# The last layer norm of a transformer block: the end of the feed-forward product in two fresh PSUM banks of 256 columns, and one of its four column blocks normalised by TensorE and ScalarE

## Chip, cores and metric

The kernel runs on one core of a Trainium2 chip. The metric is the device time of one execution in microseconds (us), median over the runs; lower is better. The engines are TensorE (PE in the profile; PEld is its weight load), VectorE (DVE), ScalarE (ACT), GpSimd (POOL) and SyncE (SP). SP, ACT and POOL also issue transfers (DMAs) from their queues.

## What is computed

One block of a hybrid network on 256 tokens of width 2048: a gated delta rule and a sparse attention, merged, then a layer norm, a gated feed-forward part of width 5632 and a second layer norm. Only the end is touched:

```python
x = layer_norm(DEEPNORM_ALPHA * x + merged @ w_out[l], ln1_g[l], ln1_b[l])
h_gate, h_up = jnp.split(x @ w_ffn_in[l], 2, axis=-1)
x = layer_norm(DEEPNORM_ALPHA * x + (jax.nn.silu(h_gate) * h_up) @ w_ffn_out[l], ln2_g[l], ln2_b[l])

def layer_norm(x, g, b):
    mu = mean(x); var = mean(square(x - mu))        # over the 2048 columns
    return (x - mu) * rsqrt(var + 1e-5) * g + b
```

Everything is f32. The large products are made of three matmuls in fp32r each: an operand is split into a high part and a rest, and hi*hi, hi*lo and lo*hi are summed.

## The kernel before

The 256 tokens are two blocks `tb` of 128 rows (partitions). The result of the second product (hidden 256 x 5632 times `w_ffn_out` 5632 x 2048) is made in two groups `g` of 1024 columns, each of two halves `n` of 512 columns; a group has four PSUM banks `bank[2 * tb + n]`. `x1[tb]` (128 x 2048, in SBUF) holds the residual and takes the sums; `out_block(tb, g, n)` is its block of 512 columns `2 * g + n`. So each row of the result has four column blocks of 512, numbered `j` from 0 to 3.

The 44 contraction tiles of 128 come as 22 pairs `q`. `chunk` (L79 to L86) loads a piece of weights of 128 x 1024 from SP's queue (L81), ScalarE casts it to `hi` (L83), and VectorE subtracts to get `lo` (L85). `mm3` (L206 to L209) is the three matmuls. Some pairs go through `seven_pair`, which makes seven products where eight would be, from forms that VectorE builds (L240 to L255); their sums are put into `x1` by `seven_chain` (L1003 to L1021) on VectorE, a step at each `tick`. The other pairs go through `plain_pair`. TensorE's and SP's order is the order of the program as written. On the other engines a scheduler sets the order by its own costs, and `tc.high_priority` moves what stands under it ahead.

In the second group the last four pairs (`HELD = 4`) are held: their products for token block 0 run first, those for token block 1 afterwards, half `n = 0` and then half `n = 1`, so that the norm of token block 0 runs on VectorE while TensorE makes block 1. The end reads:

```python
for n in range(2):                                  # L1338
    add_out(0, 1, n, bank[n])
ln2(0)
for n in range(2):
    for q, cks in held:
        for j in range(2):
            plain(bank, cks, hh_, hl_, q, j, n, 1, q == FT // 2 - 1)
    add_out(1, 1, n, bank[2 + n])
ln2(1)                                              # L1346
```

`add_out` (L1023 to L1028) adds a bank to its block of `x1` (L1025) and takes the statistics of that block (L1028, `bn_stats`, six numbers per row and block). `ln` (L1086 to L1108) aggregates them to mean and variance (`mv`, L1099), adds epsilon (`ve`, L1101), lets GpSimd raise that to the power -0.5 (`rs`, in `rsqrt`, L412), and makes for each block j two passes on VectorE: `first` (L1089), (x - mean) * gamma, and `second` (L1094), x * rs + beta. The first pass of block 0 stands ahead of `ve` in VectorE's order. Each finished block is stored at once, 256 KB, from ACT's queue for even j and SP's for odd j (L1335). `ln2_t` are four tiles of 128 x 1024 with gamma (0 and 1) and beta (2 and 3), broadcast to all rows by GpSimd's queue (L1306) during the second group.

Of the kernel before, what the change touches and what calls it, by code (L numbers as in the profile page):

```python
# [8 lines left out]
F32 = mybir.dt.float32  # L9
# [46 lines left out]
def block_kernel(ctx: ExitStack, tc: tile.TileContext, xT, x, cpack, onehot, relb, convw, alog, dtb, gnw,  # L56
# [162 lines left out]
        cs = slice(n * 512, (n + 1) * 512)  # L219
        mm3(bank[2 * tb + n], sh[:, k, ts], sl[:, k, ts], hi[:, cs], lo[:, cs], q == 0 and j == 0, last and j == 1)  # L220

    def plain_pair(bank, src, sh, sl, q, last):
        cks = pair_chunks(src, q)
        for j in range(2):
            for n in range(2):
                for tb in range(NTB):
                    plain(bank, cks, sh, sl, q, j, n, tb, last)
            tick()

    def seven_pair(bank, wbank, src, sh, sl, q, form, home, first, last):  # L230
# [46 lines left out]
    padp = ctx.enter_context(tc.tile_pool(name="padp", bufs=1, side="right"))  # L277
    pad = padp.tile([P, 24], F32, name="pad")
    nc.vector.memset(pad, 0.0)
    pads = sm.tile([P, 16], F32, name="pads")  # L280
    nc.vector.memset(pads, 0.0)
    xs_ = ExitStack()
    xpool = xs_.enter_context(tc.tile_pool(name="xp", bufs=1, side="right"))
# [714 lines left out]
    def out_block(tb, g, n):  # L998
        j = 2 * g + n
        return x1[tb][:, j * 512:(j + 1) * 512]  # L1000
# [22 lines left out]
    def add_out(tb, g, n, ps):  # L1023
        v = out_block(tb, g, n)
        nc.vector.tensor_add(v, v, ps)  # L1025
        if 2 * g + n == 0:
            stats[tb] = sm.tile([P, 4, 6], F32, name="stats", tag="stats", bufs=2)
        nc.vector.bn_stats(stats[tb][:, 2 * g + n, :], v)  # L1028

    def load_x():  # L1030
# [55 lines left out]
    def ln(tb, gt, bt, after, ahead=(0, 0, 0)):  # L1086
        def first(j):
            v = x1[tb][:, j * 512:(j + 1) * 512]
            nc.vector.scalar_tensor_tensor(v, v, mv[:, 0:1], gt[:, j * 512:(j + 1) * 512],  # L1089
                                           op0=OP.subtract, op1=OP.mult)  # L1090

        def second(j):
            v = x1[tb][:, j * 512:(j + 1) * 512]
            nc.vector.scalar_tensor_tensor(v, v, rs, bt[:, j * 512:(j + 1) * 512], op0=OP.mult, op1=OP.add)  # L1094
            after(j, v)

        with tc.high_priority(offset=ahead[0]):
            mv = sm.tile([P, 2], F32, name="mv", tag="mv", bufs=2)
            nc.vector.bn_aggr(mv, stats[tb].rearrange("p a b -> p (a b)"))  # L1099
            ve = sm.tile([P, 1], F32, name="ve", tag="ve", bufs=2)  # L1100
            nc.vector.tensor_scalar(ve, mv[:, 1:2], LN_EPS, None, op0=OP.add)  # L1101
            rs = sm.tile([P, 1], F32, name="rs", tag="rs", bufs=2)
            rsqrt(rs, ve, hv)
            first(0)
        with tc.high_priority(offset=ahead[1]):
            second(0)
        with tc.high_priority(offset=ahead[2]):
            for j in (1, 2, 3):  # L1108
                first(j)
                second(j)  # L1110
# [156 lines left out]
    def group(g, ps_std, ps_w, n):  # L1267
        nonlocal wq, mp_
        bank = [ps_std() for _ in range(4)]
        for q in range(n):  # L1270
            if not g and q == 2:
                finish()
                for i in OUT_AT:
                    h_tile(hp2, i)
                for tb in range(NTB):
                    x1[tb] = rp.tile([P, D], F32, name=f"x1_{tb}", tag=f"x1_{tb}")
                xs_.close()
                mp_ = fh.enter_context(tc.tile_pool(name="mp", bufs=1, side="right", reuse_waits="tile"))
                wq = wqs.enter_context(tc.tile_pool(name="wq", bufs=2, side="left", reuse_waits="tile"))
                for tag in ("tlo", "thi", "wt", "gt", "wraw"):  # L1280
                    wq_tile(tag)
            if q == WQ[g][0]:
                wbank = [ps_w() for _ in range(4)]
            if g and q in LN2_LOAD:
                ln2_load(LN2_LOAD.index(q))
            if not g and q in FETCH:
                fetch(OUT_AT[0] + FETCH.index(q) // 2, FETCH.index(q) % 2)
            if not g and 15 <= q < 19:
                c, tb = divmod(q - 15, 2)
                cs = slice(c * 1024, c * 1024 + 1024)  # L1290
                nc.sync.dma_start(x1[tb][:, cs], d_x1[tb, :, cs])
            if q in WQ[g]:
                seven_pair(bank, wbank, wfo[g], hh_, hl_, q, streamed, wq_tile, q == WQ[g][0], q == WQ[g][-1])
                if q == WQ[g][-1]:
                    start(seven_chain(g, wbank, mp_.tile([P, 512], F32, name="wm", tag="wm")))
            else:
                plain_pair(bank, wfo[g], hh_, hl_, q, q == FT // 2 - 1)
        return bank


# [12 lines left out]
    bank = group(1, ps_acc, ps_aux, FT // 2 - HELD)  # L1313
    wqs.close()
    ex2 = fh.enter_context(tc.tile_pool(name="ex2", bufs=4, side="left", reuse_waits="tile"))
    held = []
    for q in range(FT // 2 - HELD, FT // 2):
        cks = pair_chunks(wfo[1], q, ex2 if q < FT // 2 - HELD // 2 else None)
# [15 lines left out]
    def ln2(tb):  # L1334
        ln(tb, Halves(*ln2_t[:2]), Halves(*ln2_t[2:]), lambda j, v: (nc.sync if j % 2 else nc.scalar).dma_start(  # L1335
            out[tb * P:(tb + 1) * P, j * 512:(j + 1) * 512], v))

    for n in range(2):  # L1338
        add_out(0, 1, n, bank[n])
    ln2(0)  # L1340
    for n in range(2):
        for q, cks in held:
            for j in range(2):
                plain(bank, cks, hh_, hl_, q, j, n, 1, q == FT // 2 - 1)
        add_out(1, 1, n, bank[2 + n])
    ln2(1)  # L1346
    assert not chains
    fh.close()

# [106 lines left out]
```

## Time and profile before

| | before |
|---|---|
| median of 3 runs | 1463.47 us (1463.41 to 1463.56) |
| profiled execution | span 1462.0 us; its whole time is not recorded apart |
| TensorE busy | 1447.7 us, 99% of the span |
| VectorE, ScalarE, GpSimd busy | 1219.6, 797.0, 45.8 us |
| granted TensorE clock, mean | 0.998 |
| last store issued | 1458.74 us from the span's start |

Times in the rows of the profile count from the start of the span, which is the first to the last instruction of one execution; the runs' times also hold what lies around it. A row of the timeline is the start, the duration, the engine, the line of the source, the operation, output <- inputs and the shapes; in brackets stands how long the engine was idle before and what ended that. Rows of groups give the count, the busy time in us and the mean of one in ns. The duration of a matmul includes its way through the array, so one starts before the one ahead of it has ended.

### The profile page before, as it was taken

Reading aid. Unit: us, or ns where it says so; the run is one execution under the profiler, and the core shown is the slowest. Engines: PE = TensorE matmul, PEld = TensorE weight load, DVE = VectorE, ACT = ScalarE, POOL = GpSimd, SP = SyncE. Lnnn points to the kernel's source line nnn. Section 1 sums busy time; section 2 is a strip of 40 time slices with the busy share of each in tenths; the row PEclk is TensorE's granted clock in tenths of the full one; section 3 lists DMA queues with packets and bytes.
Section 4 is the critical chain, followed back from the end, with each engine's and each line's share of the span. In section 5 each row is a group of like instructions: output and inputs, shape, how many; then the busy total and the mean of one; then the engine's idle time right before and its main releaser. Section 6 shows DMA issues by size and latency. Waiting matters only on the chain.

```text
span 1462.0 us, 19399 instructions
## 1 busy us (share of the span) xinstructions
PE 1447.7 (99%) x7146; PEld 1217.9 (83%) x7146; DVE 1219.6 (83%) x1654; ACT 797.0 (55%) x982; POOL 45.8 (3%) x58
## 2 busy tenths in 40 slices
PE   9999999999999999999999999999999999999996
PEld 9888888888888888888888888888888888888885
DVE  6798985468489678879886799989999998989887
ACT  6765443346466445545534565656566565554551
POOL 0002010030000000000000000000000000000000
PEclk9999999999999999999999999999999999999999
DMA  8646675444556565567856767666666667888853
GB/s 295 195 155 194 185 180 169 152 135 147 186 184 217 182 208 193 185 185 245 292 182 207 239 232 245 206 211 204 228 203 211 218 215 248 311 335 267 325 199 115
DMA packets 93407, 310.16 MB, mean 212 GB/s; under 512 B 16688, under 2 KB 17624, under 8 KB 92544
## 3 DMA queue, kind: packets, MB, share of 16 engines
q1 hardware_dynamic: 82176, 290.11, 59.5%
q0 software_dynamic: 4096, 16.45, 3.5%
q10 hardware_dynamic: 7040, 2.36, 0.7%
q8 instruction: 56, 0.92, 0.3%
q14 instruction: 39, 0.32, 0.1%
HBM read 295.05 MB, written 13.83 MB: 211 GB/s over the span
## 4 chain that ended last, share of the span: by engine, by line
PE 95%; DVE 2%; DMA 1%; issue 1%; ACT 1%; SPq 0%; POOLq 0%; DVEq 0%; ACTq 0%
PE acc L145 10%; PE acc L208 10%; PE acc L209 10%; PE acc L207 10%; PE aux L207 9%; PE aux L209 9%; PE aux L208 9%; PE acc L148 5%; PE acc L167 5%; PE acc L166 5%; PE acc L165 5%; PE aux L672 1%; PE aux L165 1%; PE aux L167 1%; PE aux L166 1%
## 5 line engine op out<-in xcount | busy, mean ns | idle before, releaser
L83 ACT CAST hi<-raw 128x1024 fp32r<-128x1024 f32 (+1 forms) x391 | 405.8, 1045 | 392.1 <-PE acc L167 88.2
L85 DVE TENSOR_TENSOR lo<-raw,hi 128x1024 fp32r<-128x1024 f32 (+1 forms) x391 | 473.8, 1220 | 148.0 <-ACT hi L83 145.1
L145 PE MATMUL acc<-X,hi 128*128 128x512 f32 x640 | 203.7, 399 | 0.0
L148 PEld LDWEIGHTS acc<-X,lo 128*128 128x128 f32 x640 | 120.2, 188 | 28.3
L207 PE MATMUL acc<-hi,X 128*128 128x512 f32 x364 | 142.2, 391 | 0.0
L209 PE MATMUL acc<-hi,X 128*128 128x512 f32 x364 | 141.7, 389 | 0.0
L208 PE MATMUL acc<-lo,X 128*128 128x512 f32 x364 | 141.7, 389 | 0.0
L207 PE MATMUL aux<-hi,X 128*128 128x512 f32 x332 | 129.9, 391 | 0.6 <-DVE ol__108 L852 0.6
L209 PE MATMUL aux<-hi,X 128*128 128x512 f32 x332 | 129.3, 389 | 0.0
L208 PE MATMUL aux<-lo,X 128*128 128x512 f32 x332 | 129.2, 389 | 0.0
L148 PE MATMUL acc<-X,lo 128*128 128x256 f32 x640 | 126.0, 278 | 0.0
L145 PEld LDWEIGHTS acc<-X,hi 128*128 128x128 f32 x640 | 97.5, 189 | 2.0 <-ACT hi L83 0.7
L240 ACT CAST f_thi<-f_wt 128x1024 fp32r<-128x1024 f32 x58 | 61.1, 1054 | 52.3 <-DVE f_wt L255 30.8
L165 PE MATMUL acc<-hi,X 128*128 128x512 f32 x224 | 89.6, 400 | 0.0
L167 PE MATMUL acc<-hi,X 128*128 128x512 f32 x224 | 87.4, 390 | 0.0
L166 PE MATMUL acc<-lo,X 128*128 128x512 f32 x224 | 87.3, 390 | 0.0
L209 PEld LDWEIGHTS acc<-hi,X 128*128 128x128 f32 x364 | 68.4, 188 | 14.3
L207 PEld LDWEIGHTS acc<-hi,X 128*128 128x128 f32 x364 | 68.4, 188 | 14.0
L208 PEld LDWEIGHTS acc<-lo,X 128*128 128x128 f32 x364 | 68.3, 188 | 13.9
L241 DVE TENSOR_TENSOR f_tlo<-f_wt,f_thi 128x1024 fp32r<-128x1024 f32 x58 | 70.2, 1220 | 6.3 <-ACT f_thi L240 6.0
L207 PEld LDWEIGHTS aux<-hi,X 128*128 128x128 f32 x332 | 62.3, 188 | 13.5 <-DVE ol__108 L852 0.8
L209 PEld LDWEIGHTS aux<-hi,X 128*128 128x128 f32 x332 | 62.3, 188 | 13.0
(545 smaller groups left out, 2883.2 us busy)
## 6 DMA issues: line engine op xcount, KB each, us to landing
raw<-in_wfg_dram SPq DMA_DIRECT2D x131, 512.0 KB, 4.1
raw<-in_wws_dram SPq DMA_DIRECT2D x80, 512.0 KB, 4.1
raw<-in_wfo_dram SPq DMA_DIRECT2D x70, 512.0 KB, 5.0
raw<-in_wgt_dram SPq DMA_DIRECT2D x52, 512.0 KB, 3.6
raw<-in_win_dram SPq DMA_DIRECT2D x37, 512.0 KB, 3.7
f_wraw<-in_wfg_dram SPq DMA_DIRECT2D x29, 512.0 KB, 5.9
wraw<-in_wfo_dram SPq DMA_DIRECT2D x18, 512.0 KB, 5.1
gt<-d_g SPq DMA_DIRECT2D x18, 512.0 KB, 6.3
```

Source lines behind the costliest of these rows:

```text
L83: nc.scalar.copy(hi, raw)
L85: nc.vector.tensor_sub(lo, raw, hi.bitcast(F32))
L145: nc.tensor.matmul(pss[c], hv[:, kk, cs[c]], X2[k // 4][:, k % 4], start=(k == 0), stop=False, skip_group_check=True)
L148: nc.tensor.matmul(pss[c][:, :S], lv[:, kk, cs[c]], xh[:, k, :], start=False, stop=(k == KT - 1), skip_group_check=True)
L165: nc.tensor.matmul(ps, xh, hv[:, kk], start=(k == 0), stop=False)
L166: nc.tensor.matmul(ps, xh, lv[:, kk], start=False, stop=False)
L167: nc.tensor.matmul(ps, xl, hv[:, kk], start=False, stop=(k == 2 * n - 1))
L207: nc.tensor.matmul(o, sh, hi, start=first, stop=False)
L208: nc.tensor.matmul(o, sh, lo, start=False, stop=False)
L209: nc.tensor.matmul(o, sl, hi, start=False, stop=last)
L240: nc.scalar.copy(hi, v)
L241: nc.vector.tensor_sub(lo, v, hi.bitcast(F32))
```

## The change

Four things change in the second group and in the norm of token block 1.

First, the bank of half `n = 1` of token block 1 (`bank[3]`) is closed before the held pairs and added to its block of `x1` early (L1317 of the changed kernel). Its held products go into two fresh banks from `ps_aux()`, 256 columns each, one after the other: `held_part` makes 24 matmuls for each part. Each part is added (L1368) and has statistics of its own (L1369), so that five groups of statistics are aggregated in place of four.

Second, column block 0 of token block 1 is multiplied by gamma early (L1358), which it can be since its sum and its statistics are done by the end of the first group. Its norm is then rs * (x * gamma) + (-mean * rs) * gamma + beta. ScalarE makes a diagonal of rs (`diag`, in the tile `turn`, L1379) and a column mean * rs beside a column of -1 (`ct`, L1380). TensorE multiplies the diagonal by the block into the bank `y` (L1382), transposes `ct` to two rows (L1383), ScalarE copies these out with the sign turned (L1384), and TensorE adds the product of the two rows with the rows gamma and beta (`rows2`) to `y` (L1385). ScalarE copies `y` out (L1393) and issues its store (L1394). `rows2` is filled by two small loads on GpSimd's queue (L1355).

Third, the norm of the other three blocks stays on VectorE, with all first passes ahead of the second ones and the variance ahead of both (L1376 to L1392); their stores go from SP's queue.

Fourth, `pads` grows from 16 to 24 columns. With the larger statistics and `ct` the tiles that lie behind the pool `sm` in SBUF move by 128 bytes.

```diff
--- before.py
+++ after.py
@@ -219,12 +219,12 @@
         cs = slice(n * 512, (n + 1) * 512)
         mm3(bank[2 * tb + n], sh[:, k, ts], sl[:, k, ts], hi[:, cs], lo[:, cs], q == 0 and j == 0, last and j == 1)
 
-    def plain_pair(bank, src, sh, sl, q, last):
+    def plain_pair(bank, src, sh, sl, q, last, shut=None):
         cks = pair_chunks(src, q)
         for j in range(2):
             for n in range(2):
                 for tb in range(NTB):
-                    plain(bank, cks, sh, sl, q, j, n, tb, last)
+                    plain(bank, cks, sh, sl, q, j, n, tb, last or 2 * tb + n == shut)
             tick()
 
     def seven_pair(bank, wbank, src, sh, sl, q, form, home, first, last):
@@ -277,7 +277,7 @@
     padp = ctx.enter_context(tc.tile_pool(name="padp", bufs=1, side="right"))
     pad = padp.tile([P, 24], F32, name="pad")
     nc.vector.memset(pad, 0.0)
-    pads = sm.tile([P, 16], F32, name="pads")
+    pads = sm.tile([P, 24], F32, name="pads")
     nc.vector.memset(pads, 0.0)
     xs_ = ExitStack()
     xpool = xs_.enter_context(tc.tile_pool(name="xp", bufs=1, side="right"))
@@ -1024,7 +1024,7 @@
         v = out_block(tb, g, n)
         nc.vector.tensor_add(v, v, ps)
         if 2 * g + n == 0:
-            stats[tb] = sm.tile([P, 4, 6], F32, name="stats", tag="stats", bufs=2)
+            stats[tb] = sm.tile([P, 5, 6], F32, name="stats", tag="stats", bufs=2)
         nc.vector.bn_stats(stats[tb][:, 2 * g + n, :], v)
 
     def load_x():
@@ -1096,7 +1096,7 @@
 
         with tc.high_priority(offset=ahead[0]):
             mv = sm.tile([P, 2], F32, name="mv", tag="mv", bufs=2)
-            nc.vector.bn_aggr(mv, stats[tb].rearrange("p a b -> p (a b)"))
+            nc.vector.bn_aggr(mv, stats[tb][:, :4].rearrange("p a b -> p (a b)"))
             ve = sm.tile([P, 1], F32, name="ve", tag="ve", bufs=2)
             nc.vector.tensor_scalar(ve, mv[:, 1:2], LN_EPS, None, op0=OP.add)
             rs = sm.tile([P, 1], F32, name="rs", tag="rs", bufs=2)
@@ -1294,7 +1294,7 @@
                 if q == WQ[g][-1]:
                     start(seven_chain(g, wbank, mp_.tile([P, 512], F32, name="wm", tag="wm")))
             else:
-                plain_pair(bank, wfo[g], hh_, hl_, q, q == FT // 2 - 1)
+                plain_pair(bank, wfo[g], hh_, hl_, q, q == FT // 2 - 1, 3 if g and q == n - 1 else None)
         return bank
 
 
@@ -1313,6 +1313,8 @@
     bank = group(1, ps_acc, ps_aux, FT // 2 - HELD)
     wqs.close()
     ex2 = fh.enter_context(tc.tile_pool(name="ex2", bufs=4, side="left", reuse_waits="tile"))
+    v3 = out_block(1, 1, 1)
+    nc.vector.tensor_add(v3, v3, bank[3])
     held = []
     for q in range(FT // 2 - HELD, FT // 2):
         cks = pair_chunks(wfo[1], q, ex2 if q < FT // 2 - HELD // 2 else None)
@@ -1335,15 +1337,61 @@
         ln(tb, Halves(*ln2_t[:2]), Halves(*ln2_t[2:]), lambda j, v: (nc.sync if j % 2 else nc.scalar).dma_start(
             out[tb * P:(tb + 1) * P, j * 512:(j + 1) * 512], v))
 
+    ts1 = slice(P, S)
+
+    def held_part(ps, n, part):
+        for q, cks in held:
+            for j in range(2):
+                k = 2 * q + (j + n) % 2
+                cs = slice(n * 512 + part.start, n * 512 + part.stop)
+                hi, lo = cks[j]
+                mm3(ps, hh_[:, k, ts1], hl_[:, k, ts1], hi[:, cs], lo[:, cs], n == 1 and q == held[0][0] and j == 0,
+                    j == 1 and q == FT // 2 - 1)
+
+    gt2, bt2 = (Halves(*ln2_t[i:i + 2]) for i in (0, 2))
+    v1 = [x1[1][:, j * 512:(j + 1) * 512] for j in range(4)]
+    rows2, turn = (hp_.tile([P, 1024], F32, name=n, tag=t) for n, t in (("rows2", "hH2"), ("turn", "hL2")))
+    for i, src in enumerate((ln2g, ln2b)):
+        nc.gpsimd.dma_start(rows2[i:i + 1, :512], bass.AP(tensor=src.tensor, offset=src.offset, ap=[[0, 1], [1, 512]]))
+    ct = sm.tile([P, 2], F32, name="ct")
+    nc.gpsimd.memset(ct, -1.0)
+    nc.vector.tensor_mul(v1[0], v1[0], gt2[:, slice(0, 512)])
     for n in range(2):
         add_out(0, 1, n, bank[n])
     ln2(0)
-    for n in range(2):
-        for q, cks in held:
-            for j in range(2):
-                plain(bank, cks, hh_, hl_, q, j, n, 1, q == FT // 2 - 1)
-        add_out(1, 1, n, bank[2 + n])
-    ln2(1)
+    held_part(bank[2], 0, slice(0, 512))
+    add_out(1, 1, 0, bank[2])
+    for i in range(2):
+        part = slice(i * 256, i * 256 + 256)
+        ps = ps_aux()[:, :256]
+        held_part(ps, 1, part)
+        nc.vector.tensor_add(v3[:, part], v3[:, part], ps)
+        nc.vector.bn_stats(stats[1][:, 3 + i, :], v3[:, part])
+
+    mv = sm.tile([P, 2], F32, name="mv", tag="mv", bufs=2)
+    ve = sm.tile([P, 1], F32, name="ve", tag="ve", bufs=2)
+    rs = sm.tile([P, 1], F32, name="rs", tag="rs", bufs=2)
+    diag, ctT = turn[:, :P], turn[0:2, 512:512 + P]
+    with tc.high_priority(offset=LEAD):
+        nc.vector.bn_aggr(mv, stats[1].rearrange("p a b -> p (a b)"))
+        nc.vector.tensor_scalar(ve, mv[:, 1:2], LN_EPS, None, op0=OP.add)
+        rsqrt(rs, ve, hv)
+        nc.scalar.activation(diag, ident, AF.Copy, scale=rs)
+        nc.scalar.activation(ct[:, 0:1], mv[:, 0:1], AF.Copy, scale=rs)
+    y, a = ps_aux(), ps_aux()
+    nc.tensor.matmul(y, diag, v1[0], start=True, stop=False)
+    nc.tensor.transpose(a[0:2, :P], ct, ident)
+    nc.scalar.activation(ctT, a[0:2, :P], AF.Copy, scale=-1.0)
+    nc.tensor.matmul(y, ctT, rows2[0:2, :512], start=False, stop=True)
+    for j in (1, 2, 3):
+        nc.vector.scalar_tensor_tensor(v1[j], v1[j], mv[:, 0:1], gt2[:, slice(j * 512, j * 512 + 512)],
+                                       op0=OP.subtract, op1=OP.mult)
+    for j in (1, 2, 3):
+        nc.vector.scalar_tensor_tensor(v1[j], v1[j], rs, bt2[:, slice(j * 512, j * 512 + 512)],
+                                       op0=OP.mult, op1=OP.add)
+        nc.sync.dma_start(out[P:, j * 512:(j + 1) * 512], v1[j])
+    nc.scalar.copy(v1[0], y)
+    nc.scalar.dma_start(out[P:, :512], v1[0])
     assert not chains
     fh.close()
 
```

VectorE at the end, before: token block 1's last two adds (L1025) and statistics, the aggregate, and the norm. `x_1_10660` is `x1[1]`; `ln_0` and `ln_1` are the halves of gamma, `ln_2` and `ln_3` of beta.

```order
L1025 TENSOR_TENSOR x_1_10660<-x_1_10660,acc 128x512
L1028 BN_STATS stats<-x_1_10660 128x6
L1099 BN_AGGR mv<-stats 128x2
L1089 SCALAR_TENSOR_TENSOR x_1_10660<-x_1_10660,mv,ln_0_11748 128x512
L1101 TENSOR_SCALAR ve<-mv 128x1
L1089 SCALAR_TENSOR_TENSOR x_1_10660<-x_1_10660,mv,ln_0_11748 128x512
L1094 SCALAR_TENSOR_TENSOR x_1_10660<-x_1_10660,rs,ln_2_11932 128x512 x2
L1089 SCALAR_TENSOR_TENSOR x_1_10660<-x_1_10660,mv,ln_1_11834 128x512 x2
L1094 SCALAR_TENSOR_TENSOR x_1_10660<-x_1_10660,rs,ln_3_12018 128x512 x2
```

The same place in the changed kernel:

```order
L1368 TENSOR_TENSOR x_1_10660<-x_1_10660,aux 128x256
L1369 BN_STATS stats<-x_1_10660 128x6
L1376 BN_AGGR mv<-stats 128x2
L1377 TENSOR_SCALAR ve<-mv 128x1
L1387 SCALAR_TENSOR_TENSOR x_1_10660<-x_1_10660,mv,ln_0_11748 128x512
L1387 SCALAR_TENSOR_TENSOR x_1_10660<-x_1_10660,mv,ln_1_11834 128x512 x2
L1390 SCALAR_TENSOR_TENSOR x_1_10660<-x_1_10660,rs,ln_2_11932 128x512
L1390 SCALAR_TENSOR_TENSOR x_1_10660<-x_1_10660,rs,ln_3_12018 128x512 x2
```

Eight passes have become six, the add and the statistics ahead of the aggregate are of 256 columns, and the variance has moved ahead of the first pass.

ScalarE at the end of the changed kernel. Before, behind the last casts (L83) there were only four stores, two for each token block.

```order
L1010 COPY wm<-aux 128x512
L83 CAST hi<-raw 128x1024 x8
L1337 DMA out_dram<-x_0_10659 128x512 x2
L1379 ACTIVATE turn<-ident,rs 128x128
L1380 ACTIVATE ct<-mv,rs 128x1
L1384 ACTIVATE turn<-aux 2x128
L1393 COPY x_1_10660<-aux 128x512
L1394 DMA out_dram<-x_1_10660 128x512
```

Four operations of ScalarE and one store stand where two stores of token block 1 stood. On TensorE the products L1382, L1383 and L1385 follow the last held matmul as the program's last three.

VectorE in the held stage, as a difference (a minus is before, a plus the changed kernel): the early add between the casts' subtractions (L85) and the steps of `seven_chain`.

```order
 L1017 TENSOR_TENSOR x_0_10659<-x_0_10659,wm 128x512
 L85 TENSOR_TENSOR lo<-raw,hi 128x1024 x4
+L1317 TENSOR_TENSOR x_1_10660<-x_1_10660,acc 128x512
 L1018 TENSOR_TENSOR wm<-wm,aux 128x512
+L85 TENSOR_TENSOR lo<-raw,hi 128x1024
 L1008 SCALAR_TENSOR_TENSOR x_1_10660<-x_1_10660,wm 128x512
 L85 TENSOR_TENSOR lo<-raw,hi 128x1024
 L1021 TENSOR_TENSOR x_1_10660<-x_1_10660,wm 128x512
-L85 TENSOR_TENSOR lo<-raw,hi 128x1024 x3
+L85 TENSOR_TENSOR lo<-raw,hi 128x1024 x2
```

The add has come in behind the fourth subtraction, and the fifth has moved one step up. The other new operation of VectorE, L1358, stands in the second group between a L255 and a L241; nothing else there has moved.

## Prediction

> **What bounds the kernel now.** I read the page first, then the chain at its end, then the timelines of the last 14 us engine by engine.
>
> ```profile
> span 1462.0 us, 19399 instructions
> PE 95%; DVE 2%; DMA 1%; issue 1%; ACT 1%; SPq 0%; POOLq 0%; DVEq 0%; ACTq 0%
> ```
>
> TensorE carries 95% of the chain that ended last, VectorE 2%. The change touches the end, so the rows of that stretch decide: TensorE's held products first, then VectorE, GpSimd and the last store.
>
> ```profile
> 1445.35 0.39 PE L207 MATMUL acc<-hi,hH 128*128 128x512 f32 x1
> ...
> 1450.57 0.39 PE L209 MATMUL acc<-hi,hL 128*128 128x512 f32 x1
> 1450.99 0.69 DVE L1025 TENSOR_TENSOR x<-x,acc 128x512 f32<-128x512 f32 x1 [1.34 <-PE acc L209]
> 1451.71 0.69 DVE L1028 BATCH_NORM_STATS2 stats<-x 128x6 f32<-128x512 f32 x1
> 1452.44 0.26 DVE L1099 BATCH_NORM_AGGREGATE mv<-stats 128x2 f32<-128x24 f32 x1
> 1452.74 0.75 DVE L1089 SCALAR_TENSOR_TENSOR x<-x,mv,ln 128x512 f32<-128x512 f32 x1
> 1453.40 0.15 DVE L1101 TENSOR_SCALAR ve<-mv 128x1 f32<-128x1 f32 x1
> 1453.47 0.74 DVE L1089 SCALAR_TENSOR_TENSOR x<-x,mv,ln 128x512 f32<-128x512 f32 x1
> 1453.70 0.92 POOL L412 TENSOR_TENSOR rs<-ve,hv 128x1 f32<-128x1 f32 x1 [9.47 <-DVE ve L1101]
> 1454.65 1.41 DVE L1094 SCALAR_TENSOR_TENSOR x<-x,rs,ln 128x512 f32<-128x512 f32 x2 [0.44 <-POOL rs L412]
> 1455.98 1.41 DVE L1089 SCALAR_TENSOR_TENSOR x<-x,mv,ln 128x512 f32<-128x512 f32 x2
> 1457.31 1.41 DVE L1094 SCALAR_TENSOR_TENSOR x<-x,rs,ln 128x512 f32<-128x512 f32 x2
> 1458.74 0.33 SPq L1335 DMA_DIRECT2D out_dram<-x  x1
> ```
>
> The last 24 matmuls of 512 columns run from 1445.35 to 1450.57, 23 steps of 0.227 us. The last ends at 1450.96; from there everything is serial on VectorE (add, statistics, aggregate, eight passes of the norm, with the power on GpSimd in between) up to the last store at 1458.74; 3.26 us later the span ends. So 1458.74 is the number that the change has to move. A VectorE operation that depends on the one before starts 0.03 us after its end (1450.99 + 0.69 to 1451.71); independent norm passes follow at 0.66. GpSimd starts 0.30 after the start of the small operation that feeds it and hands on 0.03 after its end.
>
> **The change, part by part.**
>
> *Early multiply (L1358) and early add (L1317).* Both are new on VectorE, about 0.7 us each, ahead of the end. The order puts the first behind the L255 that starts at 1357.63, the second behind four L85.
>
> ```profile
> L1306 POOL DMA_DIRECT2D ln<-in_ln2g_dram x1: 545/545/545, 1347.7 to 1347.7; - x1
> DMA to landing us min/median/max: 4.5/4.5/4.5
> 1357.63 0.68 DVE L255 TENSOR_TENSOR wt<-wt,raw 128x512 f32<-128x512 f32 x1
> 1359.48 1.23 DVE L241 TENSOR_TENSOR tlo<-wt,thi 128x1024 fp32r<-128x1024 f32 x1 [1.17 <-ACT thi L240]
> 1425.06 4.62 DVE L85 TENSOR_TENSOR lo<-raw,hi 128x1024 fp32r<-128x1024 f32 x4
> 1434.98 2.49 DVE L85 TENSOR_TENSOR lo<-raw,hi 128x1024 fp32r<-128x1024 f32 x2 [0.93 <-ACT hi L83]
> 1439.43 1.37 DVE L1025 TENSOR_TENSOR x<-x,acc 128x512 f32<-128x512 f32 x2 [1.97 <-PE acc L209]
> ```
>
> The multiply needs a piece of gamma that landed at 1352.2, six us before, and falls into a hole of 1.17 us in which VectorE waits for ScalarE: no cost. The add needs the bank of the second half closed; the held stage begins 72 steps of 0.227 before the end, at 1429.0, so it is closed about when the four L85 end (1429.7), and the 0.93 idle before 1434.98 takes the 0.7 up. If either cover were gone, the products behind would come 0.7 us late on VectorE, and the hole of 1.97 says that the end of that queue had more than this to spare: between 0 and 0.7, I take 0. The two small row loads on GpSimd's queue stand behind the last load of beta and ahead of a power needed 80 us later: nothing. The other tiles move by 128 bytes: nothing that a row here could price; 0.
>
> *Product in two banks of 256.* 24 steps of 512 columns become 48 of 256, each with a weight load of its own. The first phase has such a series, with another weight at each matmul:
>
> ```profile
> 19.75 0.28 PE L131 MATMUL acc<-X,lo 128*128 128x256 f32 x1
> ...
> 22.99 0.28 PE L131 MATMUL acc<-X,lo 128*128 128x256 f32 x1
> L128 PEld LDWEIGHTS acc<-X,hi 128*128 128x128 f32 x64 | 12.3, 191 | 0.0
> ```
>
> 27 steps in 3.24 us: 0.120 each, not half of 0.227. The last start is 1445.35 + 47 x 0.120 = 1450.99, its end 0.28 later, 1451.27 instead of 1450.96: **+0.31**. The bounds of a step are 0.1135 (half a 512 step, no loss) and 0.191 (a load that hides behind nothing); I take 0.120, the same form. The Trainium skill, "TensorE: Matmul & The Clock Gate", section "LDWEIGHTS", prices a load of 128 columns at 107 ns, and its section "What overlaps and what doesn't" says that loads overlap running matmuls only when the row group differs. With a gap of 109 ns by its section "Back-to-back issue gap" that would be 216 ns a step and +4.7 us in the sum; the 0.120 here speaks against it.
>
> *Add and statistics of half the width.* At 128x256 an add out of PSUM takes 0.41 where 128x512 takes 0.68:
>
> ```profile
> L156 DVE TENSOR_TENSOR pre<-acc,half 128x256 f32<-128x256 f32 x20 | 8.0, 414 | 0.1
> L1028 DVE BATCH_NORM_STATS2 stats<-x 128x6 f32<-128x512 f32 x12 | 8.0, 684 | 0.1
> ```
>
> No statistics of 256 columns are in the trace; between half (0.34) and whole (0.68) I take 0.42 as with the add. The first part's pair runs while TensorE makes the second. Behind the last matmul: add 1451.30, statistics 1451.74, aggregate 1452.19 (one group of six more: 0.27), variance 1452.49. Two saved halves give **-0.55**. The variance no longer stands behind a norm pass: **-0.66**. Power at 1452.79, done at 1453.71; before, 1454.62: 0.91 earlier.
>
> *VectorE's branch.* Three first passes at 1452.56, 1453.22, 1453.88, three second ones at 1454.54, 1455.20, 1455.86, the last done at 1456.61, against 1458.72: -2.11. Two of the eight passes are gone, and none waits for GpSimd.
>
> *The branch of the fourth block.* ScalarE, TensorE, ScalarE, TensorE, ScalarE in turn, each waiting for the other. Nearest rows:
>
> ```profile
> L800 ACT ACTIVATE s_e<-s_e,mx 128x128 f32<-128x128 f32 x8 | 3.1, 389 | 0.0
> L496 ACT ACTIVATE kd<-kd 128x8 f32<-128x8 f32 x1 | 0.2, 194 | 0.0
> L558 ACT COPY s_t<-aux 64x256 f32<-64x256 f32 x2 | 0.7, 364 | 0.6 <-PE aux L552 0.6
> 1422.68 0.39 PE L209 MATMUL aux<-thi,gt 128*128 128x512 f32 x1
> 1423.11 0.59 ACT L1010 COPY wm<-aux 128x512 f32<-128x512 f32 x1 [2.98 <-PE aux L209]
> 42.27 0.81 PE L459 MATMUL aux<-s_e 32*8 32x384 f32 x2
> L459 PE MATMUL aux<-s_e x2: 481/482/484, 42.3 to 42.6; 32*8 32x384 f32 x2
> L1208 PE MATMUL acc<-ident,v 128*128 128x128 f32 x40 | 5.2, 273 | 0.0
> ```
>
> A plain f32 matmul is two passes in the trace: at 384 columns 0.33 between their starts and 0.48 for one, so at 512 an estimated 0.44 and 0.59, 1.03 together. Diagonal: 0.39 (128x128 with a per-partition operand), from 1453.74 to 1454.13. First matmul 1454.19 to 1455.22 (0.06 for the hand-over, estimated). Meanwhile ScalarE makes the column (0.19). The transpose issues behind the two passes, at 1455.07, ends at 1455.34 (0.27); its copy out of PSUM, half the width of the 0.364 row, estimated 0.26, ends at 1455.64 (0.04 from TensorE to ScalarE, as 1423.07 to 1423.11). Second matmul 1455.70 to 1456.73; copy 0.59 to 1457.36; store issued at 1457.38. This branch ends after VectorE's by 0.75 and sets the end: 1458.74 - 1457.38 = **-1.36**.
>
> *Bounds of the branch.* Every hand-over free and the passes at half price would put it under 1456.63, where VectorE sets the end (-2.11). Upward the open price is TensorE's clock, for the array idles here as it did not anywhere before:
>
> ```profile
> 1454.50:1455.00 0.50, 0.00 (x0) 0.00 (x0) 0.35 (x1) 0.00 (x0) 0.12 (x1) 1.00 0.00 0
> 1455.00:1455.50 0.50, 0.00 (x0) 0.00 (x0) 0.50 (x2) 0.00 (x0) 0.00 (x0) 0.62 0.00 0
> 1455.50:1456.00 0.50, 0.00 (x0) 0.00 (x0) 0.50 (x2) 0.00 (x0) 0.00 (x0) 0.50 0.00 0
> ```
>
> Each row is a stretch; the number behind the five engines' busy times is the granted clock: 1.00 until 1455.0, then half, by the 0.62 of its stretch from about 1455.12, 4.1 us after the last matmul. In the changed kernel the array is idle from 1451.27 to 1454.19, 2.9 us, then works. I take full clock, since 2.9 is under 4.1; at half clock the two passes of 0.44 take twice as long, +0.88 for each of the two matmuls.
>
> *Sum.* 1463.47 - 1.36 = **1462.1**. The profiled execution's span is 1462.0 and the median of the runs 1463.47; the 1.5 us between lie outside the span, and I leave them. The three runs lie within 0.15 us. About 0.2%, 2.9 us, is what a measurement of this kernel can tell from no change: the forecast is within that.
>
> **The rivals.**
>
> A, the forecast: the fourth block's branch sets the end at full clock, 1462.1, from 1461.7 to 1462.5 with the estimated prices.
>
> B: the clock falls inside the branch, as it does at 1455.12 now. The transpose and the second matmul then run at half: 0.1 + 0.9 = +1.0, 1463.1. For it: one matmul of 0.9 us after 2.9 idle is little activity. Against: it is activity. By the Trainium skill, same page, section "Part 1: The HAM clock gate", a fall takes a whole idle window of about 3.4 us and a rise a busy one; by that rule the 2.9 us alone do not make it fall, and once fallen it does not come back in this branch.
>
> C, slower than before: the clock is at half when the first matmul begins, so all three run at half: +1.9 on the branch, 1464.0, that is 0.5 above before. It decides if the fall comes under 2.9 us after the last matmul; the row says 4.1.
>
> D: VectorE's branch sets the end, because a pass or a hand-over is cheaper than estimated by 0.75 in all: 1461.4. For it: five hand-overs at estimated prices; against: no row shows a cheaper f32 pass.
>
> E, slower too: each 256-column step pays its weight load, 0.191. 47 x 0.071 = +3.3 us on all that follows, 1465.4. The point is a step of over 0.149 us; the series at 0.120 is the same form, so little speaks for it. The two sections of the Trainium skill named with the 256-column step are the rule that would bring it about.
>
> F: the change does nothing to the end, or costs ahead of it, because the early pair delays the split products or a shifted tile slows a stage: 1463 to 1466. The page's TensorE is at 99% with holes only of VectorE's making, which leaves little to lose.
>
> **How the numbers follow.** A 0.57, B 0.18, C 0.06, D 0.11, E 0.03, F 0.05. The time is A's. From D's lower side (1461.2) to B's upper side (1463.1 and the 0.5 that A has for its prices, 1463.6) stands 0.86; the range is 1461.2 to 1463.6. Faster by over 0.2% would need 1460.5, below D, where even VectorE's branch does not reach: 0.02. Slower by over 0.2% needs 1466.4, beyond E alone: 0.03, mostly F. Within: 0.95.
>
> **What would show it.** Right: 256-column steps of 0.12 at the end, last matmul end near 1451.3; power of the second norm starting about 1.5 us after it; two f32 matmuls of about 1.0 at granted clock 1.00; the last store from ScalarE's queue, 0.7 us behind SP's last and 1.4 earlier than before. Wrong: a granted clock of 0.5 in the rows between the two matmuls (B, C); SP's store last (D); steps of 0.19 (E); TensorE idle ahead of 1429 or the held stage starting late (F).

## The result: 12.6 us slower, and the profile after

The changed kernel takes 1476.01 us (1474.91 to 1476.62, 4 runs), against 1463.44 us (1463.21 to 1463.56, 4 runs) of the kernel before, measured beside it: ratio 1.0084, interval 1.0072 to 1.0096. The forecast was 1462.1, from 1461.2 to 1463.6. The cause was not in the norm, at which the prediction had looked closest. It was in the fourth point of the change, which the prediction had put at 0.

Two lines of the page of the changed kernel first, the span and the chain that ended last by engine:

```profile
span 1474.8 us, 19470 instructions
PE 98%; DMA 1%; ACT 0%; DVE 0%; issue 0%; POOLq 0%; SPq 0%; ACTq 0%; DVEq 0%
```

TensorE now holds 98% of the chain instead of 95%. The span is 12.8 us longer. Next, the timeline of its end (start, duration, engine, line, operation; in brackets the idle time ahead and its releaser):

```profile
1455.90 0.40 PE L207 MATMUL acc<-hi,hH 128*128 128x512 f32 x1
1456.14 0.39 PE L208 MATMUL acc<-lo,hH 128*128 128x512 f32 x1
1456.37 0.40 PE L209 MATMUL acc<-hi,hL 128*128 128x512 f32 x1
1456.61 0.39 PE L207 MATMUL acc<-hi,hH 128*128 128x512 f32 x1
1456.84 0.40 PE L208 MATMUL acc<-lo,hH 128*128 128x512 f32 x1
1457.08 0.39 PE L209 MATMUL acc<-hi,hL 128*128 128x512 f32 x1
1457.30 0.28 PE L207 MATMUL aux<-hi,hH 128*128 128x256 f32 x1
...
1462.88 0.28 PE L209 MATMUL aux<-hi,hL 128*128 128x256 f32 x1
1463.20 0.42 DVE L1368 TENSOR_TENSOR x<-x,aux 128x256 f32<-128x256 f32 x1 [0.91 <-PE aux L209]
1463.66 0.43 DVE L1369 BATCH_NORM_STATS2 stats<-x 128x6 f32<-128x256 f32 x1
1464.12 0.29 DVE L1376 BATCH_NORM_AGGREGATE mv<-stats 128x2 f32<-128x30 f32 x1
1464.44 0.15 DVE L1377 TENSOR_SCALAR ve<-mv 128x1 f32<-128x1 f32 x1
...
1464.74 0.92 POOL L412 TENSOR_TENSOR rs<-ve,hv 128x1 f32<-128x1 f32 x1 [8.65 <-DVE ve L1377]
1465.70 0.40 ACT L1379 ACTIVATE turn<-ident,rs 128x128 f32<-128x128 f32 x1 [18.17 <-POOL rs L412]
...
1466.15 2.06 PE L1382 MATMUL aux<-x,turn 128*128 128x512 f32 x2 [2.99 <-ACT turn L1379]
1466.50 2.07 DVE L1390 SCALAR_TENSOR_TENSOR x<-x,rs,ln 128x512 f32<-128x512 f32 x3
1467.27 1.66 SPq L1392 DMA_DIRECT2D out_dram<-x  x3
...
1468.78 2.07 PE L1385 MATMUL aux<-rows,turn 2*128 2x512 f32 x2 [0.35 <-ACT turn L1384]
1470.89 0.58 ACT L1393 COPY x<-aux 128x512 f32<-128x512 f32 x1 [2.16 <-PE aux L1385]
1471.50 0.34 ACTq L1394 DMA_DIRECT2D out_dram<-x  x1
```

Two things are to be seen. The last 512-column steps run from 1455.90 to 1457.08 in five steps of 0.236 us, where they took 0.227 before. And the norm's tail is no shorter: the last store is issued 8.34 us after the last product's end (1463.16), against 7.78 before. The last product ends at 1463.16 instead of 1450.96, 12.2 us later; this is nearly the whole loss, and at most 0.31 of it was forecast.

The slower steps are no matter of the end alone. Rows by stretches of 50 us show it (the bracket behind PE's busy time counts its matmuls; the number behind the five engines is the granted clock). The first two rows are the kernel before, the other two the changed one:

```profile
600.00:650.00 50.00, 50.00 (x230) 41.42 (x229) 35.22 (x39) 24.97 (x30) 0.00 (x0) 1.00 0.60 184
1350.00:1400.00 50.00, 50.00 (x222) 41.42 (x221) 45.16 (x47) 29.44 (x33) 1.07 (x2) 1.00 0.81 290
```

```profile
600.00:650.00 50.00, 50.00 (x224) 40.76 (x224) 35.26 (x39) 25.02 (x29) 0.00 (x0) 1.00 0.58 185
1350.00:1400.00 50.00, 50.00 (x217) 40.44 (x216) 45.96 (x50) 27.67 (x31) 3.15 (x6) 1.00 0.86 314
```

TensorE is busy without a gap at full clock in all four, and yet gets through 6 and 5 matmuls fewer. Nothing waits; each step is longer. A page that says "PE 99%" cannot show this.

### The profile page after: what moved, and what is told of

It reads as the page before. It is cut to its first block, busy times and chain, and to the rows that moved or that the text cites. A ratio compares the mean times of both kernels' runs of the same rounds, so it can differ in the third digit from the quotient of the medians.

```text
span 1474.8 us, 19470 instructions
## 1 busy us (share of the span) xinstructions
PE 1465.6 (99%) x7175; PEld 1221.8 (83%) x7175; DVE 1220.0 (83%) x1656; ACT 798.7 (54%) x986; POOL 46.8 (3%) x61
## 4 chain that ended last, share of the span: by engine, by line
PE 98%; DMA 1%; ACT 0%; DVE 0%; issue 0%; POOLq 0%; SPq 0%; ACTq 0%; DVEq 0%
PE acc L145 10%; PE acc L207 10%; PE acc L208 10%; PE acc L209 10%; PE aux L207 10%; PE aux L208 10%; PE aux L209 9%; PE acc L148 5%; PE acc L165 5%; PE acc L167 5%; PE acc L166 5%; DMA raw<-in_win_dram 1%; PE aux L672 1%; PE aux L165 1%; PE aux L167 1%; PE aux L166 1%
## 5 line engine op out<-in xcount | busy, mean ns | idle before, releaser
L83 ACT CAST hi<-raw 128x1024 fp32r<-128x1024 f32 (+1 forms) x391 | 405.6, 1044 | 406.1 <-PE acc L167 91.1
L85 DVE TENSOR_TENSOR lo<-raw,hi 128x1024 fp32r<-128x1024 f32 (+1 forms) x391 | 473.7, 1219 | 160.6 <-ACT hi L83 152.3
L241 DVE TENSOR_TENSOR f_tlo<-f_wt,f_thi 128x1024 fp32r<-128x1024 f32 x58 | 70.1, 1219 | 6.3 <-ACT f_thi L240 6.1
```

What stands on the lines that cost most here:

```text
L83: nc.scalar.copy(hi, raw)
L85: nc.vector.tensor_sub(lo, raw, hi.bitcast(F32))
L241: nc.vector.tensor_sub(lo, v, hi.bitcast(F32))
```

## The experiments

The theory after these rows: the tiles that moved by 128 bytes make steps longer. (Of a matmul's two inputs, the weights are the one that PEld loads, and the moving tile is the other, named first in the rows; a step is the time from one matmul's start to the next one's.) As the compiled program places them, of 5542 steps of 512 columns in fp32r before, 5482 have moving tile and weights at the same place modulo 256 bytes (they "lie alike"), and 60 don't. Of the 5518 after, 1515 don't: a shift of 128 bytes moves the hidden tiles and forms, but not the pieces of weights out of HBM and not the transposed input.

**The shift alone.** `shift128_alone` is the kernel before with one number changed:

```diff
-    pads = sm.tile([P, 16], F32, name="pads")
+    pads = sm.tile([P, 48], F32, name="pads")
```

> The kernel before with `pads` of 48 columns in place of 16: everything behind the pool `sm` lies 128 bytes further on, as in the changed kernel, and nothing else differs. Theory 1, the place in SBUF sets the step: in the changed kernel steps between 512-column matmuls whose moving tile and next weights both lie at 128 modulo 256 took 227 to 229 ns, those with one of them at 0 took 230 to 234; about 2100 steps get 3 to 7 ns longer: 1463.4 + 11.9 = 1475.3, with steps of 230 to 241 on the forms and on hH from 250 us on. Rival, the new instructions or the two smaller banks disturb the stages before: 1463.4.

Measured: 1476.16 us (1475.48 to 1476.72), ratio 1.0086, interval 1.0073 to 1.0100. One number in a tile that nothing reads makes the whole loss. The rival that the early pair or the new end delays something is out. The stretches show the same counts as the changed kernel:

```profile
600.00:650.00 50.00, 50.00 (x224) 40.76 (x224) 35.12 (x39) 25.12 (x29) 0.00 (x0) 1.00 0.55 180
1350.00:1400.00 50.00, 50.00 (x217) 40.44 (x216) 45.94 (x50) 28.22 (x30) 2.15 (x4) 1.00 0.89 319
```

**The change without the shift.** `after_shift256` is the changed kernel with the tiles 256 bytes further than before instead of 128:

```diff
-    pads = sm.tile([P, 24], F32, name="pads")
+    pads = sm.tile([P, 56], F32, name="pads")
```

> The changed kernel with `pads` of 56 columns in place of 24: all its tiles lie 256 bytes behind those of before, at the same residue modulo 256; nothing else differs. Theory 1: steps are back at 227 and the last matmul ends near 1451.3; of the change only the end is left, with the clock at half in the branch of the fourth block: last store issued 0.9 us later than before, 1464.3 (1463.9 to 1464.7). Rival, the instructions themselves cost the 12 us: 1476.

Measured: 1463.69 us (1462.63 to 1464.79, 11 runs), ratio 1.0001, interval 0.9992 to 1.0009. The loss is gone and no gain appears. The rest of the change, expected to cost 0.9 us, nets to 0.3, which can't be told from nothing; its branch ran at half clock here too, as the rows below show.

**Another common place.** The first form of the theory said that a tile has to lie at 128 modulo 256. `all_at_0` moves everything of both sides there by 128 bytes:

```diff
-    ident = cst.tile([P, P], F32, name="ident")
+    ident = cst.tile([P, P + 32], F32, name="ident")[:, :P]
...
-    pad = padp.tile([P, 24], F32, name="pad")
+    pad = padp.tile([P, 56], F32, name="pad")
```

> The kernel before with 128 bytes put in ahead of the first tile on the left and of the first on the right: every operand of TensorE lies at 0 modulo 256, none at 128. If what counts is that moving tile and weights lie alike, or that all tiles do: 1463.4. If the place itself counts: the steps with both at 0 took 230.3 in the changed kernel against 226.8, 3.5 ns on some 5500 steps: 1463.4 + 19 = 1482.

Measured: 1463.36 us (1462.65 to 1464.0), ratio 0.9999, interval 0.9990 to 1.0009. That form fell. What is left is the relative one: moving tile and weights have to lie alike.

**Half that shift.** `shift64_alone` has pads of 32 columns:

```diff
-    pads = sm.tile([P, 16], F32, name="pads")
+    pads = sm.tile([P, 32], F32, name="pads")
```

> The kernel before with `pads` of 32 columns in place of 16: everything behind `sm` lies 64 bytes further on, at 192 modulo 256. If only tiles at a multiple of 256 are slow: 1463.4. If only 128 modulo 256 is fast: as with 128 bytes, about 1475. The 60 steps of before whose weights lie at 96 modulo 256 took 233.6, which speaks for the second.

Measured: 1473.67 us (1473.20 to 1474.15), ratio 1.0070, interval 1.0056 to 1.0083. A shift of 64 bytes costs nearly as much, so there is no bad distance of just 128.

**The other side.** `right_side_128` is the kernel before with only the tiles of the right side moved, the transposed input `X2` and what lies behind it:

```diff
-    pad = padp.tile([P, 24], F32, name="pad")
+    pad = padp.tile([P, 56], F32, name="pad")
```

> The kernel before, with only the tiles of the right side (the transposed input and what lies behind it) moved by 128 bytes; forms, hidden tiles and split weights stay where they were. Theory: a step is slow where its moving tile and its weights lie at different residues modulo 256. 2988 steps of 512 columns would then be unlike that were alike: +6.2 ns each, 18.5 us, and some more for the 640 the other way round: 1482, up to 1488. Rival: only the place of the left side's tiles matters: 1463.4.

Measured: 1482.34 us (1481.10 to 1482.79), ratio 1.0124, interval 1.0110 to 1.0138: +18.4 us against 1463.9 of the kernel before, measured beside it. That this is the theory's 18.5 for the 2988 steps is in part luck. Laid step by step beside the kernel before, the two traces differ by 19.0 us, 16.2 of it in these steps (5.4 ns each); 2.1 more come from steps that still lie alike and 2.0 from steps of 256 columns. The "some more" for the 640 steps whose moving tile is the input did not come: their median is 231 ns, and it was 233 before, where they lay alike. They come in twos, between steps of 256 columns, as in these rows of the kernel before, where two of them take 0.47 us:

```profile
100.24 0.63 PE L145 MATMUL acc<-X,hi 128*128 128x512 f32 x2
100.71 0.40 PE L148 MATMUL acc<-X,lo 128*128 128x256 f32 x2
```

So lying alike is not enough for 227 in every order of steps; why these are slow is open. The loss lies where the input is used: the early stretch is short of seven matmuls, the late one, where hidden tiles that did not move are multiplied by weights that did not move, of none.

```profile
600.00:650.00 50.00, 50.00 (x223) 40.97 (x222) 37.03 (x42) 24.97 (x29) 0.00 (x0) 1.00 0.55 173
1350.00:1400.00 50.00, 50.00 (x223) 41.39 (x222) 47.34 (x53) 28.14 (x30) 2.14 (x4) 1.00 0.85 301
```

**TensorE by itself.** `grid_alone` is a kernel of its own. Its core:

```python
def run(mo, wo, n):                     # columns, 4 bytes each
    for i in range(n):
        w = wts[:, wo + i % 8 * P:wo + i % 8 * P + P]
        nc.tensor.matmul(ps[i // 3 % 4], w, mov[:, mo:mo + 512], start=True, stop=True)

for mo in (0, 32):
    for wo in range(0, 128, 8):
        run(mo, wo, 36)
```

> Computes none of the reference: TensorE alone, series of 36 matmuls of 512 columns out of tiles that nobody writes to, another weight tile at each step, for two places of the moving tile (0 and 128 modulo 256) and 16 places of the weights in steps of 32 bytes, then 12 series of alternating nines. Theory: 227 ns a step where both lie alike modulo 256, 229 to 241 where not, with some nine steps to settle after each change of place; then the same table comes out with no other engine and no DMA at work. Rival: the slow steps need the traffic of the other engines on the same tiles: 227 everywhere.

The timeline, 35 matmuls each out of five of the series; with TensorE alone, no DMA and no other engine:

```profile
90.78 8.10 PE L74 MATMUL acc<-mov,wts 128*128 128x512 f32 x35
...
191.01 8.10 PE L74 MATMUL acc<-mov,wts 128*128 128x512 f32 x35
...
107.34 8.33 PE L74 MATMUL acc<-mov,wts 128*128 128x512 f32 x35
...
124.17 8.30 PE L74 MATMUL acc<-mov,wts 128*128 128x512 f32 x35
...
140.93 8.17 PE L74 MATMUL acc<-mov,wts 128*128 128x512 f32 x35
```

The first two lie alike, both at 128 and both at 0 modulo 256: 34 steps in 8.10 less 0.39, 226.8 ns each. In the other three the moving tile lies 192, 128 and 64 bytes ahead of the weights modulo 256: 233.5, 232.6 and 228.8. All 32 series, by the mean of their last 24 steps, each distance in four series:

| moving less weights, modulo 256 | 0 | 32 | 64 | 96 | 128 | 160 | 192 | 224 |
|---|---|---|---|---|---|---|---|---|
| ns a step | 226.7 | 233.3 | 228.9 | 233.3 | 232.8 | 234.2 | 233.3 | 233.3 |

The four series of a distance agree within 0.7 ns, whether the moving tile lies at 0 or at 128. So the slow steps need no traffic of other engines, and in a long series the distance decides, not the place. One part of the expectation failed: a change of place did not cost nine steps each time. The four long series that lie alike ran at 227 from the first step, but the one of 48 at the end took nine slow steps first; of the alternating nines alike, one kind ran at 227 from the second step to the eighth, the other at 224 to 239, some 232 on average, throughout. How a series is entered matters, and by what rule stays open.

The table carries over to the whole kernel. In `shift64_alone`, 64 steps behind the fourth of a run with the distance 64 took 228.8 on average, against 228.9, and the 990 with the distance 192 took 233.3, the same as here. For the changed kernel it gives 1455 steps at 6.1 ns, 60 at about 6.8, less the 60 of before: 8.9 us of the 11.9 to be explained. Laid step by step beside the kernel before, up to the products in two banks, the traces agree: the 1455 took 9.2 us more. Another 1.7 lie in the 603 steps with both tiles at 0, of which 531 come within nine steps of a change of place (the mean of these is 230.9, of the others 226.7), and 1.9 in the 3400 with both at 128; all the rest together took 0.9 less.

**The clock.** In the changed kernel and with the 256-byte shift the f32 matmuls of the branch took 2.06 to 2.08, twice the forecast. The changed kernel by stretches of 0.5 us, then `after_shift256` by 0.25, and its first matmul of the branch in the timeline:

```profile
1465.50:1466.00 0.50, 0.00 (x0) 0.00 (x0) 0.50 (x2) 0.30 (x1) 0.16 (x1) 1.00 0.00 0
1466.00:1466.50 0.50, 0.35 (x1) 0.35 (x2) 0.50 (x1) 0.28 (x2) 0.00 (x0) 0.70 0.00 0
1466.50:1467.00 0.50, 0.50 (x1) 0.13 (x1) 0.50 (x2) 0.00 (x0) 0.00 (x0) 0.50 0.00 0
```

```profile
1453.25:1453.50 0.25, 0.00 (x0) 0.00 (x0) 0.25 (x1) 0.10 (x1) 0.12 (x1) 1.00 0.00 0
1453.50:1453.75 0.25, 0.00 (x0) 0.00 (x0) 0.25 (x2) 0.25 (x2) 0.00 (x0) 0.60 0.00 0
```

```profile
1453.85 2.08 PE L1382 MATMUL aux<-x,turn 128*128 128x512 f32 x2 [2.99 <-ACT turn L1379]
```

The 0.70 puts the fall at 1466.20, 3.04 us after the last product; the 0.60 at 1453.55, 2.68 after it (1450.87). The first matmul begins 2.99 after the last product in both: 0.30 behind the fall with the 256-byte shift, and 0.05 ahead of it in the changed kernel, so that it runs at half clock there too but for its very start. `warm_shift256` fills the hole: 13 matmuls whose result nobody reads, put between the last product and L1382 of `after_shift256`:

```diff
+    hi_w = held[-1][1][1][0]
+    for _ in range(13):
+        nc.tensor.matmul(bank[0], hh_[:, FT - 1, ts1], hi_w[:, 512:], start=True, stop=True)
     y, a = ps_aux(), ps_aux()
     nc.tensor.matmul(y, diag, v1[0], start=True, stop=False)
```

> The changed kernel with its pads grown to 56 columns (tiles 256 bytes further than before, not 128) and 13 more matmuls of 512 columns, whose result nobody reads, behind the last held one, so that TensorE isn't idle while it waits for the diagonal. If the 2.08 us of each f32 matmul in the last norm come from the granted clock having fallen in the idle 2.9 us: granted clock 1.00 in the branch, two matmuls of about 1.0 us, last store 6.1 us behind the last product (7.78 before, and products 0.31 longer): 1462.0, against 1463.7 without the 13. If a plain f32 matmul simply takes 2.07 us here, whatever ran before it: 1463.7, the matmuls still 2.07.

Its timeline (L1384 are the 13; L1385, L1388, L1396 and L1397 are L1382, L1385, L1393 and L1394 of the changed kernel) and one stretch:

```profile
1451.71 3.13 PE L1384 MATMUL acc<-hi,hH 128*128 128x512 f32 x13
...
1454.86 1.12 PE L1385 MATMUL aux<-x,turn 128*128 128x512 f32 x2
...
1456.45 1.12 PE L1388 MATMUL aux<-rows,turn 2*128 2x512 f32 x2 [0.36 <-ACT turn L1387]
1457.61 0.59 ACT L1396 COPY x<-aux 128x512 f32<-128x512 f32 x1 [1.21 <-PE aux L1388]
1458.23 0.34 ACTq L1397 DMA_DIRECT2D out_dram<-x  x1
```

```profile
1455.00:1456.00 1.00, 1.00 (x3) 0.24 (x3) 1.00 (x3) 0.00 (x0) 0.00 (x0) 1.00 0.00 0
```

At clock 1.00 the matmuls take 1.12, and the last store comes 6.36 us after the last product (1451.87) instead of 8.35 in `after_shift256`. So the clock is the cause, and nothing about the f32 matmul itself. In time: 1463.04 us (1462.31 to 1463.75, 11 runs), ratio 0.9992, interval 0.9983 to 1.0001. That is 0.86 below before where 1.4 was expected, and the interval reaches just over 1. It has the lowest median of all versions here, and it can't be called faster.

`vector_only_shift256` takes the branch out of `after_shift256`, so that all four blocks go through VectorE as before, with all first passes ahead (the early multiply and the two row loads go as well, and the stores go from both queues in turn):

```diff
-        nc.scalar.activation(diag, ident, AF.Copy, scale=rs)
-        nc.scalar.activation(ct[:, 0:1], mv[:, 0:1], AF.Copy, scale=rs)
-    y, a = ps_aux(), ps_aux()
-    nc.tensor.matmul(y, diag, v1[0], start=True, stop=False)
...
-    for j in (1, 2, 3):
+    for j in range(4):
...
-    nc.scalar.copy(v1[0], y)
-    nc.scalar.dma_start(out[P:, :512], v1[0])
```

> The changed kernel with pads of 56 columns and without the branch of TensorE and ScalarE: all four blocks of the last norm on VectorE, the second product still in two banks of 256. Last store 6.7 us behind the last product (7.78 before), products 0.31 longer: 1462.6, against 1463.7 with the branch at half clock. If the branch at half clock were no longer than VectorE's passes with all four blocks: 1463.7, the same as with the branch.

Measured: 1463.38 us (1462.91 to 1464.50), ratio 0.9997, interval 0.9988 to 1.0006: 0.5 below before where 0.8 was expected, and not to be told from it. Its end:

```profile
1453.37 2.73 DVE L1375 SCALAR_TENSOR_TENSOR x<-x,mv,ln 128x512 f32<-128x512 f32 x4
...
1456.01 2.73 DVE L1378 SCALAR_TENSOR_TENSOR x<-x,rs,ln 128x512 f32<-128x512 f32 x4
...
1457.45 1.66 SPq L1380 DMA_DIRECT2D out_dram<-x  x2
```

From the last product (1452.01) to the end of the span it takes 10.0 us, against 11.6 with the branch at half clock, 9.6 with the branch kept warm, and 11.0 before. By the profiles the simple form, VectorE alone, has all but 0.4 of what the branch can bring at its best. By the times the three can't be told from before.

## Why the prediction was wrong

**The step that failed** is the sentence "The other tiles move by 128 bytes: nothing that a row here could price; 0." It measured +12.2 us at the last product less the 0.31 of the 256-column steps, 11.9. Rival F named the mechanism's direction ("a shifted tile slows a stage: 1463 to 1466", with 0.05), but its price stopped at 2.5 us, a fifth of the loss, and its reason against, "TensorE is at 99% with holes only of VectorE's making", was no reason: the loss needed no hole. What the runs showed in place of the 0: 1455 steps more with moving tile and weights at unlike places modulo 256 bytes, some 6.3 ns longer each, and slow steps around them; `shift128_alone` makes the whole loss, and `after_shift256` takes it back.

And the sentence that no row could price it was wrong, given the places in the compiled program. Before the change, 60 steps already lay unlike, and the timeline of the kernel before shows nine of them in a row:

```profile
417.14 0.39 PE L207 MATMUL acc<-hi,X 128*128 128x512 f32 x1
417.37 0.39 PE L208 MATMUL acc<-lo,X 128*128 128x512 f32 x1
417.59 0.40 PE L209 MATMUL acc<-hi,X 128*128 128x512 f32 x1
417.83 0.39 PE L207 MATMUL aux<-g_thi,g_form 128*128 128x512 f32 x1
...
419.69 0.39 PE L209 MATMUL aux<-g_thi,g_form 128*128 128x512 f32 x1
```

Eight steps from 417.83 to 419.69 are 0.2325 us each; the same kind of matmul at the end of the kernel took 0.227. The `g_form` tiles are the ones 32 bytes off. With 1455 steps more at that price the sum would have been 1455 x 0.0055 = +8.0 us, and slower. The rows alone do not name the cause, since the 640 steps of the input are as slow and lie alike; it took the runs to tell.

**The second step that failed**, by 2 us, is "I take full clock, since 2.9 is under 4.1". The first matmul did start 2.99 after the last product, as predicted (2.92). But one fall at 4.1 is no threshold. In all ten traces the stretch at full clock is a whole number of 3413.3 ns: 1450.664 us before (425 of them), 1460.904 in the changed kernel (428), 1447.251 with the 256-byte shift (424). So in every one of them the fall came at such a mark, wherever the kernel's end lay against it: 2.3 us after the last product in `right_side_128`, 2.7 in `after_shift256`, 3.0 in the changed kernel, 3.2 in `shift64_alone`, 3.7 in `all_at_0`, 4.2 before, 4.3 in `shift128_alone`. Rival C's price is what came, in both kernels with the branch cold: the store 2.0 us later than warm, against the 1.9 it had priced. Its point, "under 2.9 us after the last matmul", was met in `after_shift256` (2.68); in the changed kernel the fall at 3.04 came 0.05 us inside the first matmul, which is rival B's condition with C's price. The Trainium skill, "TensorE: Matmul & The Clock Gate", section "Part 1: The HAM clock gate", gives a free-running window of 3413 ns; the traces agree within 3 ns over a whole span. The same section lets the clock fall after at least one idle window; here it fell with 0.7 us of matmuls inside the last 3.41 (`after_shift256`) and with 1.1 (`right_side_128`; `warm_shift256` behind its end had as much), while 1.7 us kept it up (`grid_alone`, in the window ahead of its last). By the rule in its strict form, on which rival B's odds leaned, the fall had to wait.

**What was right.** The 256-column steps took 0.119 to 0.120, +0.31. Add, statistics and aggregate took 0.42, 0.43 and 0.29 (0.41, 0.42 and 0.27 forecast), and the power starts 1.58 after the last product (1.52). Diagonal, column and copy took 0.40, 0.28 and 0.58 (0.39, 0.19 and 0.59). The early multiply and add cost nothing: from 1349.7 to the last 24 products TensorE takes the same time in `after_shift256`, which has them, as in the kernel before, within 0.01 us. At full clock the branch puts the store at 6.36 after the last product, 6.11 forecast, since an f32 matmul of 512 columns takes 1.12 there, not 1.03. With both failed steps taken away, that is `warm_shift256`, 1463.04 against 1463.9: the forecast was 1.4 less than before, measured is 0.9. Two slips in the working moved nothing: the held stage begins 96 steps before the end, not 72 (the 1429.0 is right), and steps of 216 ns would give +4.8 us, not +4.7.

## What to carry to other kernels

Before a tile is added or resized in a kernel that TensorE bounds, look where it pushes the tiles behind it: in steps like these (512 columns, fp32r, new weights each time) moving tile and weights should keep the same place modulo 256 bytes. A pad that restored this took back 12.3 us of 1476 here. Where TensorE is 99% busy, compare the number of matmuls per stretch, not the busy share: steps that got up to 3% longer show nowhere else. And before putting work on an array that has just gone idle, price it at half clock, unless something keeps the array busy: here the clock fell 2.3 to 4.3 us after the last product, by no fixed delay.

## What the runs showed of the hardware

In a long series (`grid_alone`), a 512-column fp32r step with a new weight tile each time takes 226.7 ns when both operands lie alike modulo 256 bytes, 228.9 at a distance of 64, and 232.8 to 234.2 at the other multiples of 32, with nothing else running on the chip's core. Inside the full kernel (`shift64_alone`) the two distances compared, 64 and 192, cost the same within 0.1 ns. The Trainium skill, "SBUF — State Buffer", section "Who interferes with whom", gives TensorE two independent read ports, one for the moving operand and one for the weights; if that means that the place of the one makes no difference to the other, the measured 2.8% decides against it; by what path the two meet, and whether a matmul's own weights count or the next one's, is not shown. Where steps change between the two kinds of place, those that lie alike can stay slow for up to nine steps, and the 640 steps of the input, between steps of 256 columns, took a median of 233 while they lay alike.

The granted clock stayed up for whole multiples of 3413.3 ns from its rise in all ten traces; up to 1.1 us of matmuls in the last of them did not keep it up, and 1.7 did. A plain f32 matmul of 128x512 takes 1.12 us at full clock and 2.07 at half.
